# Part of the first sides of the seven-product feed-forward moves 192 bytes within its room

## The chip, the cores and the metric

The kernel runs on one core of a Trainium2 chip. The metric is device time in microseconds (us) of one execution, lower is better; a kernel's time is the median of its runs. A core has TensorE for matmuls (PE in the profile, and PEld for its loads of weights), VectorE (DVE), ScalarE (ACT), GpSimd (POOL) and SyncE (SP), which issues transfers. On-chip memory has 128 partitions; a tile takes the same range of bytes in each of them. "Place" below means the byte at which a tile begins in a partition.

## What is computed

The reference is a trunk of four layers on 512 tokens of width 1024, in float32. Each layer adds a mixer to `x` and then a gated feed-forward network. The mixers are S5 (a diagonal state space), gated linear attention, differential attention, and S5 again.

```
h = rmsnorm(x, norm_ffn[layer])
g, u = split(h @ w_gate_up)          # 1024 x 5632, hidden width 2816
x = x + (silu(g) * u) @ w_down       # 2816 x 1024
```

## The kernel before

**Exactness.** Every float32 operand of a large matmul is split into a high part, rounded to the format that TensorE reads at speed (`F32R`), and the low rest. A product is then three matmuls: high by high, high by low, low by high. ScalarE makes the high half (`Trunk.high`, line 366) and VectorE subtracts it to get the low half (line 374). Weight tiles `whl` hold both halves, 8,192 bytes a partition, in five buffers; raw weights arrive in `wst` or in slots.

**Feed-forward by seven products.** `Trunk.ffn` cuts gate and up weights into 11 blocks of 256 columns. In each block the activations (two halves of the tokens by two halves of the width) and the weights form 2 x 2 blocks that are multiplied by Winograd's scheme with seven products in place of eight. The activations' seven combinations are called *sides*: "11", "12", "1", "2", "3", "4" and "22". They are made once in a layer and read by all 11 blocks. A product (`seven_product`, line 561) is 24 matmuls: two column groups of weights by four slices of depth by three pairs of halves. A slice of weights, 128 x 128, is the stationary operand, loaded by its own instruction; 256 tokens of a side are the moving operand. In the order of the three, the second reads the low half of the side, the first and the third its high half. In blocks 2 to 10 the products come in the order 11 (bank `a`), 1 (`c`), 2 (`a`), 12 (`d`), 3 (`a`), 4 (`c`), 22 (`a`). Blocks 0 and 1 are interleaved by a plan written out in the code (`plan`), with the sides' own making between them. The order on all engines is fixed by hand in that stretch. After every three or four blocks the down projection follows (`gemm_b`, lines 394 to 396), with the weights as the moving operand of 512 columns.

**Where the sides lie.** Sides 11 and 12 are in a tile called `sides` in `Sides.room`: 4,096 numbers a partition (16,384 bytes), that is 11 high, 11 low, 12 high, 12 low, 1,024 numbers each. It takes one buffer of a pool of two, tag `hT`; the other holds `halves`, the transposed activations, which later serve as slots for weights or as scratch. The same two buffers hold the transposed activations of the other stages (`hT0`, `hT1`, `hu`, `scr`). The other five sides are tiles of the feed-forward's own pool (`open`), each with a high and a low half of 1,024 numbers. In the profile all tiles of the room are `sides`, and those of the pool are `side`.

**Places.** Pools lie one behind the other: constants, `x`, the room's two buffers, weights, norm tiles, small statistics, and then a stage's own pool. As the program before lays them out, `sides` begins at byte 30,656 in the first three layers and at 47,040 in the last; the weight tiles begin at 63,424 and every 8,192 bytes from there; the pool's sides lie between 132,736 and 219,000. By 256, the remainder is 192 for `sides` and all its quarters, 192 for the weight tiles, and 128 for every `side` of the pool. `Trunk.edge` is a tile that nobody uses, which takes bytes so that what follows begins at another remainder.

**Statistics and tables.** Small tiles (pool `small`) have eight buffers by default, 32 bytes each: `ms2` in the readout of linear attention (line 1975), `st`, `sums` and `nm` in the attention scores (lines 2242 to 2260). `cos2` and `sin2`, the rotation tables, are constants of 64 numbers each, made in the second layer's feed-forward and read at the start of attention. `pw` is a constant of 512 numbers a partition, powers that the S5 operators need; its first 128 numbers belong to the first S5 layer.

Of the kernel before, what the change touches and what calls it, by code (L numbers as in the profile page):

```python
# [11 lines left out]
F32 = mybir.dt.float32  # L12
F32R = mybir.dt.float32r
# [3 lines left out]
ALU = mybir.AluOpType  # L17
# [4 lines left out]
P = 128  # L22
# [45 lines left out]
class Left:  # L68
# [18 lines left out]
    def room(self):  # L87
        self.hT = [self.tr.hp.tile([P, KT, SEQ], F32R, tag="hT", name=f"hT{z}") for z in range(2)]
# [72 lines left out]
class Sides(Left):  # L161
# [11 lines left out]
        return xs  # L173

    def room(self):
        F = self.tr.hp.tile([P, 4, 4, 256], F32, tag="hT", name="halves")
        self.whole = F
        self.F = {(0, 0): F[:, 0], (1, 0): F[:, 1], (0, 1): F[:, 2], (1, 1): F[:, 3]}
        two = self.tr.hp.tile([P, 2, 2, 4, 256], F32R, tag="hT", name="sides")
        self.place = {"11": two[:, 0], "12": two[:, 1]}  # L180
        self.heads = []

    def quarter(self, q, half, b):
# [9 lines left out]
    def open(self, pool, names):  # L193

        for n in names:
            self.place[n] = pool.tile([P, 2, 4, 256], F32R, name="side" + n)

    def freed(self):

        return [self.F[k] for k in ((0, 0), (0, 1), (1, 0), (1, 1))]  # L200

    def parts(self, name, src, ks=slice(0, 4)):
        o = self.place[name][:, :, ks]
        self.tr.nc.scalar.copy(o[:, 0], src)
        self.tr.nc.vector.tensor_tensor(o[:, 1], src, o[:, 0].bitcast(F32), op=ALU.subtract)

    def keep(self, t, d, p):
        for j in range(4):
# [24 lines left out]

    def high(self, name):
        for ks, y in self.of(name):
            self.tr.nc.scalar.copy(self.place[name][:, 0, ks], y)

    def low(self, name):
        for ks, y in self.of(name):
            o = self.place[name][:, :, ks]  # L240
            self.tr.nc.vector.tensor_tensor(o[:, 1], y, o[:, 0].bitcast(F32), op=ALU.subtract)


class Chunks:
# [42 lines left out]
class Trunk:  # L287
# [263 lines left out]
    def seven_product(self, side, w, bank, first, hl=None):  # L551

        if hl is None:
            hl = self.halves(w, 4, 256)
        mm = self.nc.tensor.matmul
        for j in range(2):
            c = slice(j * P, (j + 1) * P)
            o = bank[:, j * 256 : (j + 1) * 256]
            for k in range(4):
                for n, (x, y) in enumerate(((0, 0), (0, 1), (1, 0))):  # L560
                    mm(  # L561
                        o, hl[:, x, k, c], side[:, y, k], start=first and not (j or k or n),
                        stop=k == 3 and n == 2, skip_group_check=True,
                    )

# [1287 lines left out]
    def gla(self, l, left):  # L1853
# [5 lines left out]
        with self.tc.tile_pool(name="gla", bufs=1) as p:  # L1859
# [112 lines left out]
            def readout(hf, t):  # L1972
                st, o_h = sts[hf], on[hf]
                oo = row(self.tp("op"))
                ms = self.sp.tile([P, 2], F32, tag="ms2", name="ms")
                for z in range(2):
                    h = 2 * hf + z
                    zs = slice(z * 256, (z + 1) * 256)
                    for c in range(2):
                        ch = 2 * t + c  # L1980
                        nc.tensor.matmul(
                            oo[c * 64 : (c + 1) * 64, zs], qT[:, h, ch * 64 : (ch + 1) * 64], st[z][:, ch],
                            start=True, stop=True,
                        )
                for z in range(2):
                    junk = T("e")
                    nc.scalar.activation(
                        junk[:, :256], oo[:, z * 256 : (z + 1) * 256], AF.Square, scale=1.0 / 16.0,
                        accum_out=ms[:, z : z + 1],
                    )  # L1990
                r_ = self.rsqrt(ms[:], 2, 1e-6)
                for z in range(2):
                    h = 2 * hf + z
                    zs = slice(z * 256, (z + 1) * 256)
                    v.scalar_tensor_tensor(
                        o_h[:, t, zs], oo[:, zs], r_[:, z : z + 1], ng[:, h * 256 : (h + 1) * 256],
                        op0=ALU.mult, op1=ALU.mult,
                    )
# [67 lines left out]
    def diff_tables(self):  # L2066
        nc, i = self.nc, self.i
        v = nc.vector
        cp = self.cp
        self.cos2 = cp.tile([P, NT, 16], F32, name="cos2")  # L2070
        self.sin2 = cp.tile([P, NT, 16], F32, name="sin2")
        self.cidq = cp.tile([P, NT], F32, name="cidq")
        self.neglam = cp.tile([P, 1], F32, name="neglam")
        yield
        p = Slices(self.wp.tile([P, 2048], F32, tag="whl", name="dtab", bufs=5))
        if True:
            pi = p.tile([NT, P], I32, name="pi")
            nc.sync.dma_start(pi[:], i["positions"][0].rearrange("(t p) -> t p", p=P))
            ci = p.tile([NT, P], I32, name="ci")
            v.tensor_scalar(ci[:], pi[:], 6, None, op0=ALU.arith_shift_right)  # L2080
            pf = p.tile([NT, 2, P], F32, name="pf")
            v.tensor_copy(pf[:, 0], pi[:])
            v.tensor_copy(pf[:, 1], ci[:])
            yield
            yield
            yield
            ps = self.tp("pps")
            for z in range(2):
                nc.tensor.transpose(ps[:, z, :NT], pf[:, z], self.ident[:NT, :NT])
            yield  # L2090
            yield
            pos = p.tile([P, NT], F32, name="pos")
            v.tensor_copy(pos[:], ps[:, 0, :NT])
            v.tensor_copy(self.cidq[:], ps[:, 1, :NT])
            ang = p.tile([P, NT, 8], F32, name="ang")
            freq = np.float32(500000.0) ** (-np.arange(8, dtype=np.float32) / np.float32(8))
            for j in range(8):
                v.tensor_scalar_mul(ang[:, :, j], pos[:], float(freq[j]))
            yield
            red = p.tile([P, 32], F32, name="red")  # L2100
            self.reduce_angle(p, red[:], ang[:].rearrange("p t j -> p (t j)"), 32, "r")
            sn = p.tile([P, NT, 8], F32, name="sn")
            cs = p.tile([P, NT, 8], F32, name="cs")
            fl = lambda x: x[:].rearrange("p t j -> p (t j)")
            yield
            self.sincos(p, fl(sn), fl(cs), red[:], 32, "r")
            yield
            yield
            for z in range(2):
                v.tensor_copy(self.cos2[:, :, z * 8 : z * 8 + 8], cs[:])  # L2110
            v.tensor_scalar_mul(self.sin2[:, :, 0:8], sn[:], -1.0)
            v.tensor_copy(self.sin2[:, :, 8:16], sn[:])
            yield
            lm = p.tile([P, 4, 64], F32, name="lm")
            for z, s in enumerate(("diff_lam_q1", "diff_lam_k1", "diff_lam_q2", "diff_lam_k2")):
                nc.sync.dma_start(lm[:, z], i[s][0].partition_broadcast(P))
            pr = p.tile([P, 2, 64], F32, name="pr")
            lv = lm[:].rearrange("p (a b) n -> p a b n", b=2)
            v.tensor_tensor(pr[:], lv[:, :, 0], lv[:, :, 1], op=ALU.mult)
            sm = p.tile([P, 2], F32, name="sm")  # L2120
            v.tensor_reduce(sm[:], pr[:], op=ALU.add, axis=AX.X)
            ex = p.tile([P, 2], F32, name="ex")
            yield
            self.exp(p, ex[:], sm[:], 2, "l")
            yield
            v.tensor_tensor(self.neglam[:], ex[:, 1:2], ex[:, 0:1], op=ALU.subtract)
            v.tensor_scalar_add(self.neglam[:], self.neglam[:], -LAMBDA_INIT)

    def diff(self, l, left):
# [4 lines left out]
        with self.tc.tile_pool(name="diff", bufs=1) as p:  # L2134
# [90 lines left out]
            def prepare(j):  # L2225
# [13 lines left out]
                        self.nc.gpsimd.dma_start(qs[to, m], hl[rows, z, 0])  # L2239
                        self.nc.gpsimd.dma_start(ks[to, m], hl[rows, :, 1])  # L2240
                ready[j] = qs, ks
                st = self.sp.tile([P, 2, NT], F32, tag="st", name="st")
                o_s = p.tile([P, NT, P], F32, tag="o_s", name="o_s", bufs=2)
                kept[j] = st, o_s

# [2 lines left out]
            def scores(i):  # L2248
# [1 line left out]
                ts = slice(t * P, (t + 1) * P)  # L2250
                qs, ks = ready[j]
                st = kept[j][0]
                pr, sums = [], self.sp.tile([P, 4], F32, tag="sums", name="sums")
                ss = [self.sbank("s"), self.sbank("s")]
                for m in range(2):
                    for z in range(2):
                        nc.tensor.matmul(ss[m][:], qs[:, m, ts], ks[:, m, z], start=z == 0, stop=z == 1)  # L2257
                for m in range(2):
                    e = T("pr", 4)
                    nm = self.sp.tile([P, 1], F32, tag="nm", name="nm")  # L2260
                    v.tensor_tensor_reduce(  # L2261
                        e[:], ss[m][:], mask[:, t], -0.125, 3e38, op0=ALU.add, op1=ALU.min, accum_out=nm[:]
                    )
                    sum_ = st[:, 0, t : t + 1] if m == 0 else sums[:, 1:2]
                    nc.scalar.activation(e[:], e[:], AF.Exp, scale=-1.0, bias=nm[:], accum_out=sum_)  # L2265
                    pr.append(e)
# [209 lines left out]
```

## Time and profile before

| | |
|---|---|
| median of 3 runs | 2307.94 us (2307.86 to 2309.43) |
| profiled execution | 2306.32 us |
| span of its profile | 2304.6 us, 37,230 instructions |
| TensorE busy | 2218.9 us, 96% |
| VectorE busy | 1569.8 us, 68% |
| ScalarE busy | 1120.4 us, 49% |
| mean granted TensorE clock | 0.988 |

The four feed-forward layers lie at 241.5 to 583, 826 to 1132, 1448.5 to 1755 and 1954.5 to 2259 us of the span. The first also carries the making of the second S5 layer's operators.

The profile is of one execution. A group is a set of instructions of one line, engine, operation and kind of tile, with its busy time, the mean of one, and the engine's idle time just before them, with what ended it. Matmuls overlap: one is recorded as longer than the distance to the next, so the pace is read from their starts. The timeline merges neighbours of one kind into a row with a count.

### The profile page before, as it was taken

Reading aid. Unit: us, or ns where it says so; the run is one execution under the profiler, and the core shown is the slowest. Engines: PE = TensorE matmul, PEld = TensorE weight load, DVE = VectorE, ACT = ScalarE, POOL = GpSimd, SP = SyncE. Lnnn points to the kernel's source line nnn. Section 1 sums busy time; section 2 is a strip of 40 time slices with the busy share of each in tenths; the row PEclk is TensorE's granted clock in tenths of the full one; section 3 lists DMA queues with packets and bytes.
Section 4 is the critical chain, followed back from the end, with each engine's and each line's share of the span. In section 5 each row is a group of like instructions: output and inputs, shape, how many; then the busy total and the mean of one; then the engine's idle time right before and its main releaser. Section 6 shows DMA issues by size and latency. Waiting matters only on the chain. (4 is left out here: it accounts for less than half of the span.)

```text
span 2304.6 us, 37230 instructions
## 1 busy us (share of the span) xinstructions
PE 2218.9 (96%) x14847; PEld 1967.2 (85%) x14847; DVE 1569.8 (68%) x2430; ACT 1120.4 (49%) x1865; POOL 280.3 (12%) x386
## 2 busy tenths in 40 slices
PE   5889999999999999999999999999999899999997
PEld 3778979898877799998987787999999788989996
DVE  7873887776624469777745675876766964967674
ACT  5634645454452456555535675744534224635342
POOL 1000140512000010101002131111000100101000
PEclk8999999999999999999999999999999899999999
DMA  4246666664422457766337365886641546767521
GB/s 86 40 111 187 142 179 167 173 170 110 120 74 73 130 140 191 188 160 174 92 115 154 89 147 148 212 224 144 167 100 46 144 143 162 178 170 171 155 78 64
DMA packets 295319, 317.83 MB, mean 138 GB/s; under 512 B 72205, under 2 KB 235337, under 8 KB 294890
## 3 DMA queue, kind: packets, MB, share of 16 engines
q1 hardware_dynamic: 232906, 234.23, 34.1%
q0 software_dynamic: 62240, 81.22, 19.1%
q8 instruction: 117, 1.92, 0.4%
q14 instruction: 56, 0.46, 0.1%
HBM read 283.54 MB, written 16.65 MB: 130 GB/s over the span
## 5 line engine op out<-in xcount | busy, mean ns | idle before, releaser
L374 DVE TENSOR_TENSOR whl<-wst,whl 128x1024 fp32r<-128x1024 f32 x272 | 331.4, 1222 | 255.7 <-ACT whl L366 254.7
L366 ACT CAST whl<-wst 128x1024 fp32r<-128x1024 f32 x272 | 284.0, 1050 | 316.4 <-PE acc L396 227.8
L561 PE MATMUL a<-side,whl 128*128 128x256 f32 x3168 | 382.9, 277 | 4.0 <-DVE whl L374 3.0
L561 PEld LDWEIGHTS a<-side,whl 128*128 128x128 f32 x3168 | 370.3, 188 | 6.3 <-DVE whl L374 4.1
L394 PE MATMUL acc<-whl,act 128*128 128x512 f32 x704 | 278.3, 396 | 1.4 <-DVE x L544 1.4
L396 PE MATMUL acc<-whl,act 128*128 128x512 f32 x704 | 274.7, 390 | 0.0
L395 PE MATMUL acc<-whl,act 128*128 128x512 f32 x704 | 274.6, 390 | 0.0
L561 PE MATMUL c<-side,whl 128*128 128x256 f32 x2112 | 254.0, 277 | 1.2 <-DVE whl L374 1.2
L561 PEld LDWEIGHTS c<-side,whl 128*128 128x128 f32 x2112 | 246.6, 188 | 1.8 <-DVE whl L374 1.8
L374 DVE TENSOR_TENSOR whl<-slot,whl 128x1024 fp32r<-128x1024 f32 x107 | 130.5, 1222 | 70.1 <-ACT whl L366 70.1
L394 PEld LDWEIGHTS acc<-whl,act 128*128 128x128 f32 x704 | 132.1, 188 | 31.7 <-issue 2.7
L396 PEld LDWEIGHTS acc<-whl,act 128*128 128x128 f32 x704 | 132.1, 188 | 28.1
L395 PEld LDWEIGHTS acc<-whl,act 128*128 128x128 f32 x704 | 132.2, 188 | 25.6
L366 ACT CAST whl<-slot 128x1024 fp32r<-128x1024 f32 x107 | 112.2, 1053 | 85.1 <-PE acc L396 35.2
L394 PE MATMUL acc<-whl,hT 128*128 128x512 f32 x352 | 143.0, 406 | 2.5 <-DVE ro L2203 1.5
L395 PE MATMUL acc<-whl,hT 128*128 128x512 f32 x352 | 138.0, 392 | 0.9 <-DVE whl L374 0.9
L396 PE MATMUL acc<-whl,hT 128*128 128x512 f32 x352 | 138.0, 392 | 0.0
L561 PE MATMUL a<-sides,whl 128*128 128x256 f32 x1056 | 134.4, 283 | 0.0
L561 PE MATMUL d<-sides,whl 128*128 128x256 f32 x1056 | 132.8, 282 | 1.0 <-ACT whl L366 1.0
L561 PEld LDWEIGHTS a<-sides,whl 128*128 128x128 f32 x1056 | 129.7, 191 | 1.1
L561 PEld LDWEIGHTS d<-sides,whl 128*128 128x128 f32 x1056 | 128.7, 191 | 1.2 <-ACT whl L366 1.2
L700 ACT CAST act<-r 128x512 fp32r<-128x512 f32 (+1 forms) x110 | 66.3, 645 | 114.1 <-DVE r L679 107.6
(452 smaller groups left out, 3892.3 us busy)
## 6 DMA issues: line engine op xcount, KB each, us to landing
wst<-in_ffn_w_gate_up_dram SPq DMA_DIRECT2D x88, 512.0 KB, 4.6
wst<-in_ffn_w_down_dram SPq DMA_DIRECT2D x88, 512.0 KB, 4.4
slot<-in_ffn_w_gate_up_dram SPq DMA_DIRECT2D x71, 512.0 KB, 5.5
wst<-in_ffn_w_gate_up_dram POOLq DMA_DIRECT2D x44, 512.0 KB, 6.3
halves<-in_ffn_w_gate_up_dram SPq DMA_DIRECT2D x43, 512.0 KB, 5.1
wst<-in_s_w_glu_dram SPq DMA_DIRECT2D x32, 512.0 KB, 4.6
wst<-in_gla_w_in_dram SPq DMA_DIRECT2D x24, 512.0 KB, 3.7
wst<-in_diff_w_qkv_dram SPq DMA_DIRECT2D x24, 512.0 KB, 3.9
```

Of the source, the lines that this page charges most:

```text
L366: self.last["high"] = self.nc.scalar.copy(hl[:, 0], w[:])
L374: self.last["low"] = self.nc.vector.tensor_tensor(hl[:, 1], w[:], hl[:, 0].bitcast(F32), op=ALU.subtract)
L394: mm(out, lh, rh, start=first, stop=False)
L395: mm(out, lh, rl, start=False, stop=False)
L396: self.last["mm"] = mm(out, ll, rh, start=False, stop=last)
L561: mm(o, hl[:, x, k, c], side[:, y, k], start=first and not (j or k or n), stop=k == 3 and n == 2, skip_group_check=True,)
L700: self.last["act high"] = nc.scalar.copy(dst[:, 0, j], src[:, j])
```

## The change

The room's `sides` tile is allocated ahead of `halves` and has 4,224 numbers a partition in place of 4,096. The low half of side 11 lies at its beginning. Behind it 48 numbers (192 bytes) are left free; then come 11 high, 12 high and 12 low. Because `halves` has the same tag, both buffers of the pool grow by 512 bytes. The high and low half of a side are now separate views, and the functions that write and read them take them so. The bytes come from elsewhere: `cos2` and `sin2` become views of the first 128 numbers of `pw` (512 bytes), and four tags of statistics tiles have four buffers in place of eight (512 bytes). No instruction is added or removed, and no order by hand is changed. By the pools' order, `x` moves down 512 bytes, the weight and norm tiles move up 512 bytes, and what lies behind the statistics stays. `sides` begins at 47,040 in the first three layers and at 30,144 in the last. By 256, the remainder is 192 for the low half of 11 and 128 for the other three quarters.

```diff
     def room(self):
+        two = self.tr.hp.tile([P, 4224], F32R, tag="hT", name="sides")
         F = self.tr.hp.tile([P, 4, 4, 256], F32, tag="hT", name="halves")
         self.whole = F
         self.F = {(0, 0): F[:, 0], (1, 0): F[:, 1], (0, 1): F[:, 2], (1, 1): F[:, 3]}
-        two = self.tr.hp.tile([P, 2, 2, 4, 256], F32R, tag="hT", name="sides")
-        self.place = {"11": two[:, 0], "12": two[:, 1]}
+        at = lambda n: two[:, n : n + 1024].rearrange("p (k n) -> p k n", k=4)
+        self.place = {"11": (at(1072), at(0)), "12": (at(2096), at(3120))}
...
         for n in names:
-            self.place[n] = pool.tile([P, 2, 4, 256], F32R, name="side" + n)
+            y = pool.tile([P, 2, 4, 256], F32R, name="side" + n)
+            self.place[n] = (y[:, 0], y[:, 1])
...
     def parts(self, name, src, ks=slice(0, 4)):
-        o = self.place[name][:, :, ks]
-        self.tr.nc.scalar.copy(o[:, 0], src)
-        self.tr.nc.vector.tensor_tensor(o[:, 1], src, o[:, 0].bitcast(F32), op=ALU.subtract)
+        hi, lo = (y[:, ks] for y in self.place[name])
+        self.tr.nc.scalar.copy(hi, src)
+        self.tr.nc.vector.tensor_tensor(lo, src, hi.bitcast(F32), op=ALU.subtract)
...
-                        o, hl[:, x, k, c], side[:, y, k], start=first and not (j or k or n),
+                        o, hl[:, x, k, c], side[y][:, k], start=first and not (j or k or n),
...
-                ms = self.sp.tile([P, 2], F32, tag="ms2", name="ms")
+                ms = self.sp.tile([P, 2], F32, tag="ms2", name="ms", bufs=4)
...
-        self.cos2 = cp.tile([P, NT, 16], F32, name="cos2")
-        self.sin2 = cp.tile([P, NT, 16], F32, name="sin2")
+        flat = self.pw[:].rearrange("p z n s -> p (z n s)")
+        self.cos2, self.sin2 = (flat[:, z * 64 : z * 64 + 64].rearrange("p (t j) -> p t j", t=NT) for z in range(2))
...
-                st = self.sp.tile([P, 2, NT], F32, tag="st", name="st")
+                st = self.sp.tile([P, 2, NT], F32, tag="st", name="st", bufs=4)
...
-                pr, sums = [], self.sp.tile([P, 4], F32, tag="sums", name="sums")
+                pr, sums = [], self.sp.tile([P, 4], F32, tag="sums", name="sums", bufs=4)
...
-                    nm = self.sp.tile([P, 1], F32, tag="nm", name="nm")
+                    nm = self.sp.tile([P, 1], F32, tag="nm", name="nm", bufs=4)
```

`high` and `low` of the sides change as `parts` does.

More of the change, by code (lines that the diff above doesn't have):

```diff
@@ L235, in high @@
         for ks, y in self.of(name):
-            self.tr.nc.scalar.copy(self.place[name][:, 0, ks], y)
+            self.tr.nc.scalar.copy(self.place[name][0][:, ks], y)
     def low(self, name):
         for ks, y in self.of(name):
-            o = self.place[name][:, :, ks]
-            self.tr.nc.vector.tensor_tensor(o[:, 1], y, o[:, 0].bitcast(F32), op=ALU.subtract)
+            hi, lo = (z[:, ks] for z in self.place[name])
+            self.tr.nc.vector.tensor_tensor(lo, y, hi.bitcast(F32), op=ALU.subtract)
 class Chunks:
```

## The prediction

> **What bounds the kernel now.** I read the page's busy shares first, to see whether one engine is the bound all the way.
>
> ```profile
> PE 2218.9 (96%) x14847; PEld 1967.2 (85%) x14847; DVE 1569.8 (68%) x2430; ACT 1120.4 (49%) x1865; POOL 280.3 (12%) x386
> ```
>
> TensorE is busy for 96% of the span. The change touches tiles of the four feed-forward layers, so next I read busy time by stage. The columns are the stretch, its length, then busy time and count for PE, PEld, DVE, ACT and POOL, the granted clock, the DMA share and GB/s.
>
> ```profile
> 241.50:583.00 341.50, 339.92 (x2746) 308.30 (x2745) 266.46 (x409) 174.79 (x291) 98.77 (x148) 1.00 0.59 152
> 826.00:1132.00 306.00, 303.66 (x2251) 287.18 (x2249) 243.84 (x364) 171.55 (x243) 33.27 (x35) 1.00 0.61 158
> 1448.50:1755.00 306.50, 304.14 (x2250) 287.81 (x2249) 230.40 (x267) 153.81 (x205) 28.21 (x24) 1.00 0.64 162
> 1954.50:2259.00 304.50, 303.26 (x2249) 287.49 (x2248) 219.19 (x245) 145.20 (x185) 24.24 (x19) 1.00 0.57 144
> ```
>
> In each layer TensorE lacks only 1.2 to 2.4 us of the whole stretch, at a granted clock of 1.00, while DVE is idle for 62 to 85 us and the DMA engines are about 60% busy. A shorter matmul there is time off the end. Third, the groups of instructions at line 561, the one matmul of all seven products (mean ns of one behind the bar's first number).
>
> ```profile
> L561 PE MATMUL a<-side,whl 128*128 128x256 f32 x3168 | 382.9, 277 | 4.0 <-DVE whl L374 3.0
> L561 PEld LDWEIGHTS a<-side,whl 128*128 128x128 f32 x3168 | 370.3, 188 | 6.3 <-DVE whl L374 4.1
> ...
> L561 PE MATMUL a<-sides,whl 128*128 128x256 f32 x1056 | 134.4, 283 | 0.0
> L561 PE MATMUL d<-sides,whl 128*128 128x256 f32 x1056 | 132.8, 282 | 1.0 <-ACT whl L366 1.0
> L561 PEld LDWEIGHTS a<-sides,whl 128*128 128x128 f32 x1056 | 129.7, 191 | 1.1
> ```
>
> The same instruction on the same shape is 6 ns longer, and its weight load 3 ns longer, when the moving operand is `sides` (first sides 11 and 12, in the room) than when it is a `side...` tile of a pool. Matmuls overlap, so what counts is the distance between starts. The timeline of TensorE in one block, merged by product (start us, us, engine, line, tiles, count):
>
> ```profile
> 365.04 3.02 PE L561 MATMUL a<-sides,whl 128*128 128x256 f32 x24
> 367.90 2.90 PE L561 MATMUL c<-side,whl 128*128 128x256 f32 x24
> 370.64 2.88 PE L561 MATMUL a<-side,whl 128*128 128x256 f32 x24
> 373.36 3.02 PE L561 MATMUL d<-sides,whl 128*128 128x256 f32 x24
> 376.23 2.90 PE L561 MATMUL a<-side,whl 128*128 128x256 f32 x24
> 378.96 2.88 PE L561 MATMUL c<-side,whl 128*128 128x256 f32 x24
> 381.68 2.88 PE L561 MATMUL a<-side,whl 128*128 128x256 f32 x24
> 384.40 0.87 PE L561 MATMUL a<-sides,whl 128*128 128x256 f32 x6
> ```
>
> From start to start, a product on `sides` takes 2.86 or 2.87 us, the one behind it 2.74 or 2.73, and every other 2.72. No gap separates them, so this difference is TensorE's own. Two longer runs give the steady pace:
>
> ```profile
> 247.75 5.92 PE L561 MATMUL d<-sides,whl 128*128 128x256 f32 x48
> 253.51 5.62 PE L561 MATMUL c<-side,whl 128*128 128x256 f32 x48
> 258.97 3.11 PE L561 MATMUL a<-side,whl 128*128 128x256 f32 x24
> ```
>
> 48 matmuls on `sides` take 5.76 us, 120 ns each; the next 48 take 5.46, 113.8 each. The pool's tiles start at a remainder of 128 bytes by 256, the room's at 192, and the weight tiles at 192. So the slow pairs are those in which both operands of TensorE start at one remainder. The change puts both halves of 12 and the high half of 11 at 128; the low half of 11 stays at 192.
>
> **The change part by part.**
>
> *Side 12, wholly moved.* It then looks like a pool tile: the pair of this product and its follower goes from 2.87 + 2.73 = 5.60 us to 2 x 2.72 = 5.44, a gain of 0.16 us. There is one pair in each of 11 blocks of 4 layers, 44 in all.
>
> *Side 11, half moved.* Of each three matmuls two read the high half and one the low half. No row shows such a mixture. Bounds for the pair: at worst it stays at 5.60 (no gain), at best it falls to 5.44 (gain 0.16). Between them I go by how the pace changes at the borders: a product on `sides` takes 2.86 although 24 x 0.120 is 2.88, and its follower 2.74 against 2.72, so about 0.02 us of the excess arrives late and is carried over. One matmul in three in the slow place then gives about a third of 0.14, 0.04 to 0.05. I take 2.76 for the product and 2.73 for its follower, a gain of 0.11.
>
> *What of it counts.* In the body of a layer nothing else holds TensorE. The first two blocks are interleaved, with DVE closer behind, and in block 2 the stretch is DVE's:
>
> ```profile
> 282.00:292.00 10.00, 8.76 (x69) 8.04 (x69) 10.00 (x14) 7.80 (x13) 1.34 (x1) 1.00 0.55 107
> ```
>
> ```profile
> 281.94 3.20 PE L561 MATMUL a<-sides,whl 128*128 128x256 f32 x24
> 284.98 0.40 PE L561 MATMUL c<-side,whl 128*128 128x256 f32 x2
> 285.77 2.79 PE L561 MATMUL c<-side,whl 128*128 128x256 f32 x22 [0.39 <-DVE whl L374]
> ```
>
> Here DVE is busy for all 10.00 us, and product 1 stops after two matmuls for the low half of its weights. What 11 saves in block 2, and part of what blocks 0 and 1 save, becomes a longer wait there. I count these at half: bounds nothing and all, since DVE itself waits for weight tiles that TensorE frees. The sum:
> - 12 in blocks 2 to 10: 36 x 0.16 = 5.8 us
> - 11 in blocks 3 to 10: 32 x 0.11 = 3.5 us
> - the starts: 12 x 0.11 + 8 x 0.16 = 2.6, half is 1.3 us
>
> Together 10.6 us. The profiled execution took 2306.32 us (span 2304.6); less 10.6 that is 2295.7. The median of the runs, 2307.94, lies 1.6 above it, so the forecast on the median's scale is **2297.3 us**.
>
> *Edits counted at nothing.* The room's tiles change buffers, because `sides` is now allocated ahead of `halves`. The rows of the first layer show what cover there is:
>
> ```profile
> L1470 PE MATMUL y<-scr,prods x256: 275/275/421, 60.6 to 164.6; 128*128 128x128 f32 x128
> ...
> L209 ACT ACTIVATE halves<-tp,gffn x128: 347/374/440, 197.0 to 1959.1; 128x128 f32<-128x128 f32 x128
> ...
> L204 ACT CAST sides<-halves x8: 1047/1052/1097, 200.4 to 1952.8; 128x1024 fp32r<-128x1024 f32 x8
> ...
> L1098 DVE TENSOR_TENSOR halves<-halves,pw x32: 347/388/428, 310.0 to 528.9; 128x256 f32<-128x256 f32 x16, 128x192 f32<-128x192 f32 x16
> ```
>
> The old contents of these buffers are last read at 164.6, and the first writes come at 197.0 and 200.4, so either order leaves over 30 us. The tables that now lie in `pw` are written in the second feed-forward layer, behind 826 us, and the last reader of `pw` ends at 529: about 300 us of cover. The statistics tiles go from 8 buffers to 4. The nearest wait is `nm`: its fifth writer needs the exponential of two score steps before.
>
> ```profile
> L2261 DVE CUSTOM_DVE_ANT_0 pr<-s,mask 128x512 f32<-128x512 f32 x64 | 42.2, 686 | 30.1 <-PE s L2257 30.0
> ```
>
> ```profile
> L2265 ACT ACTIVATE pr<-pr,nm x64: 705/723/733, 1243.1 to 1411.8; 128x512 f32<-128x512 f32 x64
> ```
>
> The instruction that makes `nm` also writes `pr`, which already has four buffers and is freed later still, by the transposes of that step; so the wait adds nothing, and what DVE waits for there is TensorE's scores (30.0 us). Without that cover each of 32 steps could lose one exponential, 32 x 0.72 = 23 us. Instructions and transfers stay the same in number.
>
> **The rivals.**
>
> *The first side stays slow.* If one slow matmul in three is enough to keep TensorE in the slow pace, 11 gains nothing: 36 x 0.16 + half of 8 x 0.16 = 6.4 us, 2301.5. For it: a slow product carries its excess into the next one. Against it: that excess is gone within 0.02 us.
>
> *The byte is not the cause.* All fast tiles lie behind byte 132,000 of a partition, all slow ones ahead of byte 64,000, so the place in the memory separates them as well as the remainder does. If it is the place, 192 bytes change nothing: 2307.9. Against it: the load of weights lengthens too (191 against 188), although these tiles are the same in both kinds of product.
>
> The Trainium skill, "SBUF — State Buffer", section "Who interferes with whom", says that TensorE reads its moving operand and its weights through two independent ports and never waits on anyone; by that rule where the two operands start would not matter, and the time would stay at 2307.9. Line 561's rows do not agree with it as it stands: TensorE's pace on `sides` and on `side` differs with no releaser named.
>
> *Slower: the weight tiles.* The pools ahead of them lose 512 bytes and the room gains 1024, so all weight tiles move up 512 bytes. The 512-column matmuls read them as the moving operand:
>
> ```profile
> L396 PE MATMUL acc<-whl,act 128*128 128x512 f32 x704 | 274.7, 390 | 0.0
> ...
> L396 PE MATMUL acc<-whl,hT 128*128 128x512 f32 x352 | 138.0, 392 | 0.0
> ```
>
> With lines 394 and 395, which have the same counts, that is 3 x (704 + 352) = 3168 matmuls. At line 561's price, 6 ns each, they would lose 19 us, which less the 10.6 gained gives 2316.3. It decides from 3.4 ns each. For it: no row has these tiles at the new place. Against it: the weight slices of a product at line 561 alternate in steps of 512 bytes and keep one pace.
>
> **How the numbers follow.** Chances: the forecast 0.66, the first side staying slow 0.12, the byte not being the cause 0.14, the weight tiles 0.08. A difference of 0.2%, 4.6 us, is about what a measurement of this kernel can tell from no change. The first two cases are faster (0.78), the third is the same (0.14), the fourth slower (0.08). The forecast's own range has all 88 pairs at 0.16 (14.1 us, 2293.8) at one end and only the 36 sure pairs (5.8 us, 2302.2) at the other. For 8 in 10 I reach 2 us below it and up to the case of no effect: 2292 to 2308.
>
> **What would show it.** At line 561 the group d<-sides should come to 277 ns with loads of 188, and its product in a block to 2.72 us between starts; a<-sides should lie between, at 2.76 (2.72 to 2.86). The products behind both should lose their 0.02. The wait on DVE in block 2 should grow by up to 0.1 us. Rows 394 to 396 should keep 390 to 396 ns, and DVE's idle time ahead of `pr` its 30 us. The prediction is wrong if d<-sides keeps 282, if rows 394 to 396 lengthen, or if the four layers shorten while another stage grows.

## The result and the profile after

The median after the change is **2319.38 us** (2317.53 to 2322.66, 6 runs), before 2307.90 us (2305.83 to 2312.27, 6 runs). The ratio is 1.0047, with an interval of 1.0034 to 1.0060: the change makes the kernel 11.5 us **slower**. The forecast was 10.6 us faster, and its range ended at 2308. The profiled execution took 2319.64 us, with a span of 2317.9 us and a mean granted TensorE clock of 0.989 (0.988 before).

The two places of `sides` after the change, given ahead of the prediction, are the wrong way round. In the compiled program `sides` lies at 30,144 in the first three layers and at 47,040 in the last; the two buffers of the room did not swap. The remainders by 256 are as stated: 192 for the low half of 11, 128 for the other three quarters, 192 for the weight tiles. Lines of the changed kernel are two higher: 561 is now 563, and 394 to 396 are 396 to 398.

The busy shares of the changed kernel, from the page:

```profile
PE 2231.7 (96%) x14847; PEld 1980.1 (85%) x14847; DVE 1569.4 (68%) x2430; ACT 1119.3 (48%) x1865; POOL 280.2 (12%) x386
```

TensorE is busy 12.8 us longer with the same 14,847 matmuls; the other engines are where they were. The four feed-forward stretches next, cut from the first to the last matmul of the seven products, first the sum row of before and then the changed kernel (columns as in the prediction):

```profile
sum 1255.90, PE 1248.37 PEld 1168.40 DVE 957.30 ACT 644.67 POOL 184.49; mean PE 312.09 PEld 292.10 DVE 239.32 ACT 161.17 POOL 46.12
```

```profile
242.90:585.70 342.80, 340.90 (x2743) 309.16 (x2742) 265.66 (x408) 174.40 (x291) 98.72 (x148) 1.00 0.59 151
830.90:1139.20 308.30, 305.85 (x2248) 289.24 (x2247) 243.27 (x364) 170.85 (x243) 33.27 (x35) 1.00 0.60 156
1456.10:1764.40 308.30, 306.37 (x2245) 290.02 (x2243) 229.54 (x266) 154.07 (x205) 28.21 (x24) 1.00 0.63 161
1964.20:2271.80 307.60, 306.11 (x2246) 290.30 (x2245) 218.95 (x244) 144.53 (x185) 24.24 (x19) 1.00 0.56 143
sum 1267.00, PE 1259.22 PEld 1178.72 DVE 957.43 ACT 643.85 POOL 184.45; mean PE 314.81 PEld 294.68 DVE 239.36 ACT 160.96 POOL 46.11
```

The stretches are 11.1 us longer (1267.0 - 1255.9), which is nearly all of the 11.5, and TensorE's busy time in them grows by 10.9. The granted clock is 1.00 in all of them, as before. So the time is lost where the prediction wanted to gain it. The groups of TensorE's instructions by tile:

```profile
L563 PE MATMUL a<-side,whl 128*128 128x256 f32 x3168 | 392.1, 280 | 3.9 <-DVE whl L376 3.7
...
L398 PE MATMUL acc<-whl,act 128*128 128x512 f32 x704 | 274.6, 390 | 0.0
...
L563 PE MATMUL a<-sides,whl 128*128 128x256 f32 x1056 | 133.1, 282 | 0.0
L563 PE MATMUL d<-sides,whl 128*128 128x256 f32 x1056 | 129.7, 280 | 1.0 <-ACT whl L368 1.0
```

The surprise is in the rows that the change does not touch. Products on the pool's tiles, `side`, went from 277 to 280 ns, though neither these tiles nor their remainders moved. `d<-sides`, which moved, went only from 282 to 280, where 277 was forecast. The 512-column matmuls at line 398 kept 390.

A mean of 280 hides two values. The timeline of TensorE in one block of the changed kernel (start us, us, engine, line, tiles, count):

```profile
366.71 3.02 PE L563 MATMUL a<-sides,whl 128*128 128x256 f32 x24
369.57 2.90 PE L563 MATMUL c<-side,whl 128*128 128x256 f32 x24
372.31 2.88 PE L563 MATMUL a<-side,whl 128*128 128x256 f32 x24
375.03 2.88 PE L563 MATMUL d<-sides,whl 128*128 128x256 f32 x24
377.75 2.88 PE L563 MATMUL a<-side,whl 128*128 128x256 f32 x24
```

and in a later one, behind the next down projection:

```profile
449.38 2.99 PE L563 MATMUL c<-side,whl 128*128 128x256 f32 x24
452.20 2.99 PE L563 MATMUL a<-side,whl 128*128 128x256 f32 x24
455.03 2.99 PE L563 MATMUL d<-sides,whl 128*128 128x256 f32 x24
457.86 2.99 PE L563 MATMUL a<-side,whl 128*128 128x256 f32 x24
460.68 2.99 PE L563 MATMUL c<-side,whl 128*128 128x256 f32 x24
```

In the first block product 12 and the pool's products take 2.72 us from start to start, as forecast, and product 11 takes 2.86 (369.57 - 366.71). In the second, the very same instructions on the very same tiles take 2.82 to 2.83 us each, with no gap between them. So TensorE has **two steady paces for one product**: 2.720 us (113.3 ns a matmul) and 2.827 us (117.8 ns). I call them fast and slow. The steps at single matmuls, in ns from start to start and read from the trace, tell them apart:

```
fast:  113 113 114 113 ...               loads of weights 188
slow:  117 118 118 117 118 118 118 ...   loads of weights 188 188 192, in turn
all operands at 192 (before): 120 ...
```

The pace can be read for 218 of an execution's 220 pool products (products on a `side` tile). At the slow pace are 5 of them before, and 154 after. The price of it: a block of seven takes 2 x 5.60 + 3 x 2.72 = 19.36 us before (the prediction's rows), 7 x 2.827 = 19.79 in the slow pace, and 2.86 + 2.73 + 5 x 2.72 = 19.19 in the fast one after the change. By the trace 31 of the 44 blocks are slow: 31 x 0.43 - 13 x 0.17 = +11.1 us, against +11.1 in the stretches and +11.5 in the medians. **This accounts for the result**; the open question is why the slow pace comes in, and why it did not before.

### The profile page after: what moved, and what is told of

Same layout as the page of the kernel before. It is cut to its first block, busy times and chain, and to the rows that moved or that the text cites. A ratio compares the mean times of both kernels' runs of the same rounds, so it can differ in the third digit from the quotient of the medians.

```text
span 2317.9 us, 37231 instructions
## 1 busy us (share of the span) xinstructions
PE 2231.7 (96%) x14847; PEld 1980.1 (85%) x14847; DVE 1569.4 (68%) x2430; ACT 1119.3 (48%) x1865; POOL 280.2 (12%) x386
## 5 line engine op out<-in xcount | busy, mean ns | idle before, releaser
L563 PE MATMUL a<-side,whl 128*128 128x256 f32 x3168 | 392.1, 280 | 3.9 <-DVE whl L376 3.7
L563 PEld LDWEIGHTS a<-side,whl 128*128 128x128 f32 x3168 | 378.7, 189 | 6.7 <-DVE whl L376 5.5
L563 PE MATMUL c<-side,whl 128*128 128x256 f32 x2112 | 260.1, 280 | 1.4 <-DVE whl L376 1.3
L563 PEld LDWEIGHTS c<-side,whl 128*128 128x128 f32 x2112 | 252.1, 189 | 2.2 <-DVE whl L376 2.2
```

The lines of the kernel that those rows point to most:

```text
L563: mm(o, hl[:, x, k, c], side[y][:, k], start=first and not (j or k or n), stop=k == 3 and n == 2, skip_group_check=True,)
```

## The experiments

The theory to be tested: before, TensorE could fall into the slow pace as well, but the two products in which all of the side lay at 192 brought it back twice in each block. The change took both away. A *restart* below is a place where something interrupts the row of products: a down projection, transposes, or a wait for halves. The rivals: the mixture of two remainders in product 11 brings the slow pace in; the layout around it does (weights and `x` moved by 512 bytes, tables, statistics); or the quarters' remainder of 128 is simply a bad one in the room. Runs e1 to e4 shared one chip and the runs of before (27, median 2307.55 us), e5 to e8 another set (14, 2306.71), e9 and e10 a third (19, 2308.68). The stage ahead of the first feed-forward layer varies by itself by 6 us (the first of these matmuls starts between 239.8 and 246.1 us in the profiled executions), so beside the median I give the sum of the four stretches of the profiled execution, from first to last matmul of the seven products. The last column counts pool products at the slow pace.

| run | median us (range, runs) | ratio to before [interval] | sum of stretches us | slow |
|---|---|---|---|---|
| before | 2307.90 (2305.83 to 2312.27, 6) | | 1255.9 | 5 of 218 |
| the change | 2319.38 (2317.53 to 2322.66, 6) | 1.0047 [1.0034, 1.0060] | 1267.0 | 154 of 218 |
| e1, all moved | 2314.19 (2309.85 to 2316.66, 10) | 1.0032 [1.0019, 1.0044] | 1264.6 | 131 of 218 |
| e2, none moved | 2307.39 (2302.26 to 2310.88, 10) | 0.9993 [0.9981, 1.0005] | 1255.0 | 1 of 218 |
| e3, only 12 moved | 2303.54 (2299.55 to 2306.23, 9) | 0.9974 [0.9963, 0.9986] | 1250.6 | 7 of 218 |
| e4, high half of 11 at 192 | 2300.26 (2296.27 to 2305.71, 7) | 0.9966 [0.9949, 0.9983] | 1249.3 | 9 of 218 |
| e5, one slice of 11 at 192 | 2300.78 (2299.03 to 2304.67, 8) | 0.9970 [0.9958, 0.9981] | 1247.5 | 13 of 218 |
| e6, order in 11 | 2318.84 (2312.53 to 2322.04, 6) | 1.0045 [1.0028, 1.0062] | 1264.4 | 135 of 218 |
| e7, all at 0 | 2321.76 (2317.24 to 2324.01, 4) | 1.0057 [1.0037, 1.0078] | 1268.3 | 166 of 218 |
| e8, all at 64 | 2317.22 (2315.74 to 2317.86, 5) | 1.0044 [1.0027, 1.0061] | 1264.8 | 112 of 218 |
| e9, six matmuls ahead | 2307.08 (2301.14 to 2313.29, 10) | 0.9992 [0.9978, 1.0006] | 1250.8 | 1 of 216 |
| e10, two matmuls ahead | 2305.74 (2303.36 to 2307.61, 10) | 0.9989 [0.9979, 0.9999] | 1252.7 | 35 of 218 |

All edits are on the changed kernel. The pair of numbers for a side is where its high and its low half begin in the room's tile, counted in float32 numbers.

### e1: all four quarters at remainder 128

```diff
-        self.place = {"11": (at(1072), at(0)), "12": (at(2096), at(3120))}
+        self.place = {"11": (at(48), at(1072)), "12": (at(2096), at(3120))}
```

> All four quarters of the first sides begin at a remainder of 128 bytes by 256; the rest is as in the changed kernel. Theory A (TensorE has two steady paces for the same product, 113.3 and 117.8 ns a matmul, and it is the product with its two halves at different remainders that tips it into the slower one): nothing tips it, all seven products take 2.72 us, the 44 pairs gain 0.16 us each against before, and the time is 2308 - 7 - 7 = 2294 us. Theory B (any pause tips it, and a product that runs wholly at 120 ns, as both did before, is what brings it back): nothing brings it back any more, the products take 2.83 us each, and a block takes 7 x 2.827 = 19.79 us against 2 x 5.60 + 3 x 2.72 = 19.36 before: 2308 + 44 x 0.43 = 2327 us.

Measured 2314.19 us, 6.6 slower than before. There is no mixture left, no operand of a side shares a remainder with the weights, and yet 131 products run slow. The timeline of e1, where before has 2.72 and 2.86 in turn:

```profile
368.50 2.99 PE L563 MATMUL c<-side,whl 128*128 128x256 f32 x24
371.32 2.99 PE L563 MATMUL a<-side,whl 128*128 128x256 f32 x24
374.15 2.99 PE L563 MATMUL d<-sides,whl 128*128 128x256 f32 x24
376.98 2.99 PE L563 MATMUL a<-side,whl 128*128 128x256 f32 x24
```

The mixture is not what brings the slow pace in. In this kernel the pace never changes inside an unbroken row of products, either way: each change stands at a restart. In an execution 59 products 11 and 12 stand in an unbroken row between two pool products; here, and in the changed kernel too, all 59 leave the pace as they find it. Of nine restarts behind a projection, eight come out slow and one fast, in both kernels. The time lies between the two forecasts (2294 and 2327), because not every block is slow. The sum agrees with the count: with every product fast the gain would be 2 x 0.16 us in each of 44 blocks, 14.1; the 26 slow blocks cost 7 x 0.107 = 0.75 each, 19.5. That makes +5.4, against +6.6 in the medians and +8.7 in the stretches.

### e2: the change's layout, with all quarters at 192

```diff
-        self.place = {"11": (at(1072), at(0)), "12": (at(2096), at(3120))}
+        self.place = {"11": (at(0), at(1024)), "12": (at(2048), at(3072))}
```

> The wider room, its place, the tables and the statistics tiles are as in the changed kernel, and the four quarters lie side by side from the room's beginning as before, all at a remainder of 192. Theory A: as before, 2308 us, products on the first sides at 2.86 us and all others at 2.72 or 2.74. Theory C (the weight tiles' move by 512 bytes, or the tables and buffers, cost the time): slower, 2316 to 2325 us.

Measured 2307.39 us, the time of before within the interval. The timeline of e2 has the steps of before:

```profile
367.84 3.02 PE L563 MATMUL a<-sides,whl 128*128 128x256 f32 x24
370.70 2.90 PE L563 MATMUL c<-side,whl 128*128 128x256 f32 x24
373.44 2.88 PE L563 MATMUL a<-side,whl 128*128 128x256 f32 x24
376.16 3.02 PE L563 MATMUL d<-sides,whl 128*128 128x256 f32 x24
```

All nine restarts behind a projection come out fast. So the larger tile, weights 512 bytes further on, the tables in `pw` and the smaller statistics pools cost nothing that shows. The 12.0 us between this kernel and the change come from the places of three quarters alone.

### e3: only side 12 moves

```diff
-        self.place = {"11": (at(1072), at(0)), "12": (at(2096), at(3120))}
+        self.place = {"11": (at(0), at(1024)), "12": (at(2096), at(3120))}
```

> Side 11 stays at 192 with both halves, side 12 lies at 128 with both. Theory A: 11 takes 2.86 us and its follower 2.74, as before, all others 2.72; 44 pairs gain 0.16 us, 2308 - 7 = 2301 us. Theory B: the same, since 11 brings the pace back once in every block; a pause behind it can leave some products of a block at 2.83, which gives up to 2305.

Measured 2303.54 us, 4.0 faster than before, and 5.3 less in the stretches; 44 x 0.16 = 7.0 was the most there could be. The groups of e3 on the room's tiles:

```profile
L563 PE MATMUL a<-sides,whl 128*128 128x256 f32 x1056 | 134.5, 283 | 0.0
...
L563 PE MATMUL d<-sides,whl 128*128 128x256 f32 x1056 | 126.7, 276 | 1.0 <-ACT whl L368 1.0
```

`d<-sides` comes to 276 ns: the prediction's step for 12 holds, **as long as 11 stays at 192 and brings TensorE back once in a block**. One product that is slow in itself keeps the other six fast. In the last layer its return can be seen in an unbroken row: block 2 ends at the slow pace, and the products behind the next 11 are at 2.72 to 2.74 us.

### e4: the high half of 11 at 192 in place of the low one

```diff
-        self.place = {"11": (at(1072), at(0)), "12": (at(2096), at(3120))}
+        self.place = {"11": (at(0), at(1072)), "12": (at(2096), at(3120))}
```

> The high half of 11 stays at 192 and its low half lies at 128, the reverse of the changed kernel; 12 lies at 128. Theory A, if any mixture tips the pace: most products at 2.83 us, about 2319 us as in the changed kernel. Theory A, if it takes one slow matmul in three to tip it: no product at 2.83 behind this 11, which itself takes 2.8 to 2.86, and 2300 to 2302 us. Theory B: 2301 to 2319, by how often a pause falls behind 11.

Measured 2300.26 us, 7.3 faster than before. The timeline of e4:

```profile
362.82 2.99 PE L563 MATMUL a<-sides,whl 128*128 128x256 f32 x24
365.64 2.90 PE L563 MATMUL c<-side,whl 128*128 128x256 f32 x24
368.38 2.88 PE L563 MATMUL a<-side,whl 128*128 128x256 f32 x24
```

Product 11 takes 2.83 us and its follower 2.73, against 2.86 and 2.73 in the change's fast blocks. All nine restarts behind a projection come out fast, and no slow pool product is left in blocks 3 to 10. So a mixture as such is harmless. With two of three matmuls at 192 TensorE leaves 11 at the fast pace there; with the one that reads the low half it does not. But it is not certain to: the 9 slow pool products are all product 1 in blocks 0 to 2 of three layers, and in blocks 0 and 1 they stand behind 11 and 12 without a break. The timeline of e4 in the first layer:

```profile
246.00 5.82 PE L563 MATMUL d<-sides,whl 128*128 128x256 f32 x48
251.65 5.82 PE L563 MATMUL c<-side,whl 128*128 128x256 f32 x48
```

The 48 matmuls of 12, which lies at 128, take 5.65 us, the slow pace, directly behind 11. Swapping the two halves of 11 is worth 19 us (2319.38 to 2300.26).

### e5: one slice of depth of 11's high half at 192

```diff
-        self.place = {"11": (at(1072), at(0)), "12": (at(2096), at(3120))}
+        self.first = two[:, 0:256].unsqueeze(1)
+        rest = two[:, 304:1072].rearrange("p (k n) -> p k n", k=3)
+        self.place = {"11": ([self.first[:, 0], *(rest[:, k] for k in range(3))], at(1072)), "12": (at(2096), at(3120))}
...
+            for hi, part in ((self.first, slice(0, 1)), (self.rest, slice(1, 4))):
+                self.tr.nc.scalar.copy(hi, src[:, part])
+            for hi, part in ((self.first, slice(0, 1)), (self.rest, slice(1, 4))):
+                self.tr.nc.vector.tensor_tensor(lo[:, part], src[:, part], hi.bitcast(F32), op=ALU.subtract)
```

The high half is written in two parts, so there is one more copy and one more subtraction in a layer.

> As the kernel with all quarters moved, but the first of the four depth slices of 11's high half lies at a remainder of 192, so 4 of the 24 matmuls of product 11 read the slow place (written by one copy and one subtraction more in each layer). Theory B (a stretch in the slow place brings TensorE back from the slower pace, in every block): product 11 takes 2.74 to 2.80 us, all other products 2.72, and the time is 2294 + 44 x 0.02 to 0.08 = 2295 to 2298 us. If four such matmuls are too few, the pace stays as with all quarters moved: about 26 of 44 blocks at 2.83 us a product, 2314 us.

Measured 2300.78 us, 5.9 faster than before; the stretches are the shortest of all, 8.4 less than before. The timeline of e5, whose lines are ten higher:

```profile
369.33 2.94 PE L573 MATMUL a<-sides,whl 128*128 128x256 f32 x24
372.11 2.88 PE L573 MATMUL c<-side,whl 128*128 128x256 f32 x24
374.83 2.88 PE L573 MATMUL a<-side,whl 128*128 128x256 f32 x24
```

Product 11 takes 2.78 us and everything behind it 2.72. The steps of this 11 in ns, from the trace, with a bar between its two column groups: `119 118 118 122 115 115 113 ... | 119 118 118 121 116 114 114 113 ...`. Each group begins with two matmuls at 192 among three; after steps of 118 and 119 and one of 121 or 122 TensorE is down at 113. Twice 11 follows a pool product at the slow pace in an unbroken row, and the slow pace ends within it: at 1512.35 us in the first group, at 890.84 only in the second (`... 120 117 118 118 117 119 117 118 | 121 115 115 122 116 114 113 ...`). So four of the 24 at 192 are enough, and all nine restarts behind a projection come out fast. The median lies 3 us above the forecast range (2295 to 2298); the paragraph on the starts below says where part of that went.

### e6: another order of the three matmuls in 11

Places as in e1; in product 11 the low half of the side is read last.

```diff
-                for n, (x, y) in enumerate(((0, 0), (0, 1), (1, 0))):
+                for n, (x, y) in enumerate(((0, 0), (1, 0), (0, 1)) if last_low else ((0, 0), (0, 1), (1, 0))):
```

> As the kernel with all quarters moved, but in product 11 the three matmuls of a slice come in the order high by high, low weights by high side, high weights by low side. If the slower pace hangs on the order in which the halves' addresses follow one another, product 11 ends it in every block: 2.72 us for the other products and about 2294 us. If it is only a matter of where two streams stand to one another, the order changes nothing: 2314 us as with all quarters moved.

Measured 2318.84 us, with 135 slow products against 131 in e1 and nearly the same sum of the stretches (1264.4 against 1264.6). This order inside product 11 neither brings the slow pace in nor ends it.

### e7 and e8: all quarters at remainder 0, and at 64

```diff
-        self.place = {"11": (at(1072), at(0)), "12": (at(2096), at(3120))}
+        self.place = {"11": (at(16), at(1040)), "12": (at(2064), at(3088))}      # e7
+        self.place = {"11": (at(32), at(1056)), "12": (at(2080), at(3104))}      # e8
```

> All quarters of 11 and 12 begin 64 bytes behind the old place, at a remainder of 0 by 256. If only the remainder of 192, equal to that of the weights, is slow and brings TensorE back: as with all quarters moved, 2314 us. If a remainder of 0 is slow as well, 11 and 12 take 2.8 to 2.9 us and bring TensorE back: about 2308. If it is fast and brings it back: 2294.

> All quarters of 11 and 12 begin 128 bytes behind the old place, at a remainder of 64 by 256. The same three cases: 2314 us if it is like 128, about 2308 if it is like 192, 2294 if products there are fast and bring TensorE back.

Measured 2321.76 us (e7) and 2317.22 us (e8), both slower than before. A slow sequence in e7, across the border of two blocks:

```profile
567.23 2.99 PE L563 MATMUL a<-side,whl 128*128 128x256 f32 x24
570.05 2.99 PE L563 MATMUL a<-sides,whl 128*128 128x256 f32 x24
572.88 2.99 PE L563 MATMUL c<-side,whl 128*128 128x256 f32 x24
```

At remainder 0 products 11 and 12 take 2.83 us themselves and do not end the slow pace. They do not bring it in either: in the few fast blocks of e7 they take 2.83 us too, and the pool's products behind them 2.72. All 59 in an unbroken row leave the pace as they find it; none of the three cases named beforehand has this. At 64 it is another picture. A block in e8:

```profile
366.02 3.01 PE L563 MATMUL a<-sides,whl 128*128 128x256 f32 x24
368.87 2.91 PE L563 MATMUL c<-side,whl 128*128 128x256 f32 x24
371.62 2.88 PE L563 MATMUL a<-side,whl 128*128 128x256 f32 x24
374.34 3.01 PE L563 MATMUL d<-sides,whl 128*128 128x256 f32 x24
377.19 2.99 PE L563 MATMUL a<-side,whl 128*128 128x256 f32 x24
```

Both products on `sides` take 2.85 us. Behind 11 TensorE comes back to 2.72, behind 12 it goes over to 2.83. That is not a matter of which side it is. In a block of the third layer it is the other way round:

```profile
1515.82 2.88 PE L563 MATMUL a<-side,whl 128*128 128x256 f32 x24
1518.54 3.01 PE L563 MATMUL a<-sides,whl 128*128 128x256 f32 x24
1521.39 2.99 PE L563 MATMUL c<-side,whl 128*128 128x256 f32 x24
...
1527.04 3.01 PE L563 MATMUL d<-sides,whl 128*128 128x256 f32 x24
1529.89 2.91 PE L563 MATMUL a<-side,whl 128*128 128x256 f32 x24
1532.64 2.54 PE L563 MATMUL c<-side,whl 128*128 128x256 f32 x21
```

At 64 a product **reverses** the pace that it finds: all 59 in an unbroken row do, 24 from slow to fast and 35 from fast to slow, without a restart. Since 11 and 12 take turns, 12 mostly undoes what 11 did. Of the remainders tried, 192 for at least part of 11's high half is the only one that kept the slow pace away.

### e9 and e10: matmuls at 192 ahead of product 11, with places as in e1

```diff
+                for k in range(6):          # 2 in e10
+                    nc.tensor.matmul(bank["a"][:, :256], h[:, 0, k % 4, :P], h[:, 0, k % 4], start=True, stop=True)
```

They stand ahead of product 11 in the first block behind each projection, nine places. They read weights, which lie at 192, as both operands, and nothing uses what they compute.

> As the kernel with all quarters moved, with six more matmuls of 256 columns ahead of product 11 in the first block behind a down projection (9 places in the program). They read the weights themselves as the moving operand, which lie at a remainder of 192, into a bank that product 11 then starts anew; they compute nothing that is used. If TensorE comes into the slower pace at the restart behind a projection, keeps it until something ends it, and a few matmuls in the slow place end it: the products of all groups behind a projection take 2.72 us, and the four layers' products and projections together become shorter than with all quarters moved by 2 groups or 3 a layer of slow blocks less 9 x 0.7 us, about 1264.6 - 18 + 6 = 1252 us; the median about 2302 us. If the pace is not a state that TensorE carries, they only cost: 1271 us, median 2320.

> The same with two such matmuls. If two are enough to end the slower pace: the four layers' products and projections come to about 1264.6 - 18 + 2 = 1249 us, the median to about 2299. If they are too few: between 1258 and 1267 us, the median 2309 to 2317.

In the profiled execution of e9 the nine restarts come out fast, and so do all but one of the pool products. The timeline of e9 at the second of them:

```profile
444.04 0.87 PE L635 MATMUL a<-whl 128*128 128x256 f32 x6
444.75 2.90 PE L563 MATMUL a<-sides,whl 128*128 128x256 f32 x24
447.48 2.88 PE L563 MATMUL c<-side,whl 128*128 128x256 f32 x24
450.20 2.88 PE L563 MATMUL a<-side,whl 128*128 128x256 f32 x24
```

The stretches take 1250.8 us, 13.8 less than e1 though they hold 9 x 0.71 = 6.4 us of added matmuls. The median, 2307.08, is 7.1 below e1's, from another set of runs, but 5 above the forecast of 2302 and not told apart from before: the ten runs lie between 2301.1 and 2313.3, and the profiled one (2301.24) is at the lower end. I take it that in other executions some restarts still come out slow, but no profile of such a one was taken, so this is not shown. In e10 two such matmuls were too few at two of the nine restarts, both in the first layer (30 slow pool products in the six blocks behind them; the other 5 of the 35 stand ahead of the first projection), and the seven others came out fast; 2305.74 us, 1252.7 in the stretches, between the two forecasts. Both fit the theory that matmuls with both operands at 192 end the slow pace and need not belong to a side. No run put the same added matmuls at another remainder, so that it is their place and not the added work is not shown by these two runs alone.

## Why the prediction was wrong, point by point

**The step that failed** is the one for side 12: "It then looks like a pool tile". It took the 2.72 us of the pool's products as a property of their place. The rows bore that out, but only because each block held two products that brought TensorE back to that pace. The change took away both, one wholly and one in the part that mattered, and the slow pace then held through whole groups of blocks: behind a projection all nine restarts come out fast before, in e2, e3, e4 and e5, and eight of nine slow in the change and in e1. The part's answer to "what holds TensorE in the body of a layer" looked only at waits; TensorE's own pace, as something carried from one instruction to the next, was not among the terms or the rivals. The word "carried" was there, for 0.02 us at the borders: that was the tail of this very return (steps of 121, 122, 115, 115, then 113 in the product behind one at 192), read as a leftover.

**The sum's terms, in a fast block.** Side 12's 0.16 us is right: 2.72 in the fast block of the change, and 276 ns in e3. Side 11's 0.11 was too much: the mixed product takes 2.86 us, as before, and its follower 2.73. That is no gain; the rival "the first side stays slow" had this part right, and gave 2301.5. With 13 fast blocks of 44 neither could be seen in the time.

**The rival on the byte** falls. e2 and the change have the same layout but for the remainders of three quarters, and differ by 12.0 us. What the Trainium skill says on its page "SBUF — State Buffer", section "Who interferes with whom", is that TensorE's two read ports are independent. Read as the prediction read it, that where the two operands start would not matter, it does not agree with e2 and the change, nor with 120 ns at 192 against 113.3 at 128 for one shape.

**The slower rival,** the weight tiles, gave 2316.3 us, close to the measured time, and was wrong all the same. The rows at lines 396 to 398 kept 390 to 396 ns for `act`, and e2 has the weights at their new place and the time of before. The rows for `hT` read 3 ns more (395 for 392 at line 398), but with the weights at the same new place e4 has 392 again, so this is not the place. A time that fits is no proof of its mechanism; the rows were.

**Edits counted at nothing.** They cost nothing that shows, although the room's tiles did not change buffers as the prediction says. DVE's wait for the scores ahead of `pr` is 31.0 us after, 30.1 before:

```profile
L2263 DVE CUSTOM_DVE_ANT_0 pr<-s,mask 128x512 f32<-128x512 f32 x64 | 42.2, 686 | 31.0 <-PE s L2259 30.9
```

The wait in block 2, forecast to grow by up to 0.1 us, went from 0.39 to 0.45. The timeline of the changed kernel there:

```profile
286.29 0.40 PE L563 MATMUL c<-side,whl 128*128 128x256 f32 x2
287.13 2.86 PE L563 MATMUL c<-side,whl 128*128 128x256 f32 x22 [0.45 <-DVE whl L376]
```

**The starts, counted at half.** Cut at product 11 of block 3 of each layer, the traces show where the smaller variants gained. Blocks 3 to 10 became 4.8 us (e3), 5.8 (e4) and 8.8 (e5) shorter, of 5.1, 6.4 and 8.5 by the terms for one pair (by the trace 11's pair gains 0.04 in e4 and 0.106 in e5). Blocks 0 to 2 gave only 0.5, 0.9 and -0.4 of 1.9, 2.4 and 3.2. So half was too much for the starts, and this is where most of the sums 44 x 0.16 = 7.0, 44 x 0.20 = 8.8 and 44 x 0.266 = 11.7 fell short in the stretches (5.3, 6.6, 8.4). That waits for DVE take it back there was argued and not tested.

**What would have shown it before.** The slow pace is in the trace of before: 5 of its 218 pool products run at it, each behind a restart. A view of the pool's products one by one, not their mean of 277 ns, would have raised the question what ends it. All five end at another restart. But the trace also holds a return without one: in block 2 of the third layer 22 matmuls of product 2, behind a wait, run slow from 1497.77 us, product 12, at 192, follows without a break, and the product behind it comes down to 113 ns.

**What stays open.** Why a restart behind a down projection so often comes out slow; why four matmuls of the high half at 192 reset the pace (e5) while the eight of the low half in the change do not, and why e4's sixteen do not in blocks 0 and 1 of three layers; and why a product at 64 reverses the pace. The weights lay at a remainder of 192 in every run, so whether 192 itself counts or only that both operands share a remainder was not tested. Nor do the runs show that 256 bytes is the period: by 512, the weights and the old `sides` both lie at 448.

## What to carry to other kernels

Where an engine runs back to back, the mean of a group can hide two paces, so read the distances between starts over whole sequences before a product's time is taken as its own. Before a slow piece is removed, ask what the pieces behind it would do without it: here one slice of 256 columns kept at the slow place (e5), or the halves of 11 the other way round (e4), is 0.3% faster than before, and the fully moved sides are 0.3% slower. When only places in memory change, run the same layout with the old places first (e2): that one run takes away every rival that lies in the layout around them.

## What the runs showed of the hardware

For matmuls of 128x128 weights by 256 columns in the `F32R` format, with weights at remainder 192 by 256 bytes, TensorE has three steady paces at a granted clock of 1.00. It takes 120 ns when the moving operand begins at 192 as well; with the moving operand at 128 it takes 113.3 or 117.8. Which of the last two depends on what ran before. It persists through all seven products of a block and across blocks, and all 59 products on `sides` in unbroken rows pass it on (e1). A restart behind a projection brought the slow one in eight times of nine there. Matmuls with both operands at 192 end it, four of 24 in e5 (behind a whole product at 192, four steps of 115 to 122 ns later TensorE is at 113), but in e4 sixteen of 24 did not always. In the slow one every third load of weights takes 192 ns instead of 188. With the moving operand at remainder 0 a product takes 117.8 ns a matmul at either pace and passes the pace on (59 of 59 in e7); at 64 it takes about 118.7 and reverses it (59 of 59 in e8).
